# A convolution's bias in its band matrices, LayerNorm's affine part on VectorE, and fewer early query loads

## The chip, the cores and the metric

One core of a Trainium2 chip. The metric is the device time of one execution in microseconds (us), the median over several runs. Engines: TensorE (PE; its weight loads PEld), VectorE (DVE), ScalarE (ACT), GpSimd (POOL) and SyncE (SP), which here issues nearly all transfers; a few are issued by ACT and POOL.

## The reference, cut to what matters

The program is one step of a two-layer hybrid network on 256 prompt tokens and 1024 sample tokens of width 1024. Layer 0 projects the normed input to a convolution branch (A) and a differential attention (B). The change is in branch A:

```python
a = a_u * jax.nn.sigmoid(a_g)                      # 512 channels
a = lax.conv_general_dilated(a, conv_w, ..., feature_group_count=A_W) + conv_b   # 31 taps, one filter per channel
a = jax.nn.silu(layer_norm(a, ln_g, ln_b)) * jax.nn.silu(a_z)
# layer_norm: (x - mean) * rsqrt(var + 1e-6) * g + b over the 512 channels
...
return jnp.concatenate([a, o], axis=-1) @ w_out    # o: the attention's output
```

All tensors are float32; products are made of two parts, a rounded value (`hi`) and what is left of it (`lo`).

## The kernel before, in words

`l0_in` is the input projection of layer 0. Seven groups of 512 weight columns pass over ten tiles of 128 tokens; after each unit, `filler` calls the steps of two generators, so that their work stands between the projection's matmuls: `branch` (the convolution `conv`, then `ln_steps`) and `mod` (the modulation of later stages, on DVE).

The first group writes `a` times 2, as `hi` and `lo`, to the DRAM buffers `AW` (L410 to L420), with zero rows between and around the two sequences (L404 to L408). `conv` takes 64 channels at a time, `q` = 0 to 7. `windows(q)` (L432) makes a tile `X` of 128 partitions: partitions 0 to 63 hold 64 consecutive time steps of `hi`, 64 to 127 those of `lo`, for 42 overlapping windows that start every 32 steps. Four transfers fill it (even and odd windows, `hi` and `lo`), each of 64 rows x 21 windows x 64 channels, on SP's queue. Two `X` tiles take turns (`bufs=2`): the load of window `q+1` is called at `c0 == 8` of window `q` (L463) and has to wait until the matmuls of window `q-1` are through. Each channel's matmul (L471) multiplies its column of `X` with a band matrix of 64 rows x 32 outputs that is built on the host in `_layout` from the 31 taps (L1522 to L1526); an output of the 32 needs 31 steps, so rows 0 to 61 are used and rows 62 and 63 of each half are zero. The band matrices (`rawb`, `band`) of 16 channels are loaded two ahead (`load_taps`, `cut_taps`), on the same queue. The result goes to PSUM, is summed by ACT and DVE (L476, L477) into `cy`, and is stored by ACT's queue to `CV` (L480).

`ln_steps` takes ten tiles of `CV`: `stats` halves the value and adds the bias (L575), takes mean and variance (L577, L579), adds the epsilon (L580), raises to the power -1/2 on POOL (L95) and makes the factor and the offset (L582); `norm` applies them on ACT (L587) and multiplies and adds the affine part on POOL (L588, L589); then come Tanh on ACT (L610) and two products on DVE (L593, L594), and the store to `CAT`. Its tiles take over the memory of the `X` tiles and of `cy`.

`freed0` (L1418) is called in the last weight group: it opens the pool `pre0` on the memory of the first sample tokens' input and loads the keys of head 0 (`l0_keys`) and the queries of groups 1, 2 and 0 of head 0 (`l0_query`, four transfers each), all on SP's queue. `l0_attn` takes those queries at L782 and loads all others when it comes to them, from a pool with three buffers.

The order of the instructions on each engine and queue is made by a planner at build time, from the program's order as priority and estimated durations; each engine and each queue then runs its list in order.

Of the kernel before, what the change touches and what calls it, by code (L numbers as in the profile page):

```python
# [10 lines left out]
F32 = mybir.dt.float32  # L11
F32R = mybir.dt.float32r
BF16 = mybir.dt.bfloat16
AF = mybir.ActivationFunctionType
ALU = mybir.AluOpType
# [8 lines left out]
EPS = 1e-6  # L24
CW0 = 288
CWIN = 42
CROWS = 32 * CWIN + 32
CCH = 64
# [4 lines left out]
def f32(ap):  # L33
    return ap.bitcast(F32)
# [42 lines left out]
class K:  # L77
# [323 lines left out]
    def l0_in(self, ws, raw, wp, cxp, p1, small, acc, pst, mod, freed):  # L401
        nc, a = self.nc, self.a
# [7 lines left out]
        def ug_units(gi):  # L410
# [10 lines left out]

            return [(f"ug{gi}_{t}", self.mm_tok(t), lambda ps, t=t: done(t, ps)) for t in TORD]

        def conv():

# [2 lines left out]
            raws, bands = [], []  # L430

            def windows(q):  # L432
                x = cxp.tile([128, CWIN, CCH], F32R, tag="X", bufs=2, name=f"X{q}")
                cs = slice(q % 4 * CCH, q % 4 * CCH + CCH)
                for o in range(2):
                    for hl in range(2):
                        src = self.AW[q // 4][hl, 32 * o : 32 * o + 32 * CWIN, cs].rearrange("(j r) c -> r j c", r=64)
                        dst = x[hl * 64 : hl * 64 + 64].rearrange("p (j o) c -> p o j c", o=2)[:, o]
                        nc.sync.dma_start(f32(dst), f32(src))
                return x  # L440

# [17 lines left out]
            for q in range(8):  # L459
                y = cxp.tile([CWIN, 32, CCH], F32, tag="cy", bufs=1, name=f"cy{q}")  # L460
                x = xs.pop(0)
                for c0 in range(0, CCH, 8):
# [3 lines left out]
                    for i in range(8):  # L466
                        c = c0 + i
                        if c % 16 == 0:
                            cut_taps()
                        w = bands[4 * q + c // 16]  # L470
# [7 lines left out]
                    if c0 + 8 == CCH:  # L478
                        dst = self.CV[:, q * CCH : q * CCH + CCH].rearrange("(w m) c -> w m c", m=32)
# [3 lines left out]
        def head_units(h):  # L483
# [21 lines left out]
                            nc.sync.dma_start(f32(dst).rearrange("i c t -> (i c) t"), f32(x[qk * 64 : qk * 64 + 64, hl, 0:n]))  # L505

            def vz_done(t, ps):
                v = small.tile([128, 128], F32, tag="vz", name=f"vz{h}_{t}")
                nc.scalar.copy(v, ps[:, 256:384])
                nc.sync.dma_start(self.V0[h, t], v)  # L510
                gz = small.tile([128, 128], F32, tag="gz", name=f"gz{h}_{t}")
                self.silu2(gz, ps[:, 384:512], small, f"z{h}_{t}")
                nc.vector.tensor_tensor(gz, gz, self.subg, ALU.mult)
                nc.sync.dma_start(self.GZ0[h, t], gz)
                return v
# [30 lines left out]
            vz = [(f"v{h}_{t}", self.mm_tok(t, 256), lambda ps, t=t: vz_done(t, ps)) for t in range(NT)]  # L546
# [10 lines left out]
        def ln_steps():  # L557

            con = cxp.tile([128, 3, 512], F32, tag="cy", bufs=1, name="lncon")
            for i, nm in enumerate(("lng", "lnb", "convb")):
                nc.sync.dma_start(con[:, i], a[nm].broadcast_to([128, 512]))
            ws = [cxp.tile([128, CWIN * CCH], F32, tag="X", bufs=2, name=f"lnw{i}") for i in range(2)]
            slots = [w[:, i * 512 : i * 512 + 512] for w in ws for i in range(5)]
# [6 lines left out]

            def stats(t):
                u = us[t % 6]
                nc.vector.scalar_tensor_tensor(u, u, 0.5, con[:, 2], ALU.mult, ALU.add)  # L575
                st = small.tile([128, 6], F32, tag="bn", name=f"bn{t}")
                nc.vector.bn_stats(st, u)  # L577
                mvs[t] = mv = small.tile([128, 4], F32, tag="mv", bufs=3, name=f"mv{t}")
                nc.vector.bn_aggr(mv[:, 0:2], st)  # L579
                nc.vector.tensor_scalar(mv[:, 1:2], mv[:, 1:2], EPS, None, ALU.add)  # L580
                self.rsq(mv[:, 2:3], mv[:, 1:2])
                nc.vector.tensor_scalar(mv[:, 3:4], mv[:, 0:1], mv[:, 2:3], -1.0, ALU.mult, ALU.mult)  # L582

            def norm(t):
                u, mv = us[t % 6], mvs[t]
                nc.sync.dma_start(azs[t % 2], self.AZ[t])
                nc.scalar.activation(u, u, AF.Identity, bias=mv[:, 3:4], scale=mv[:, 2:3])  # L587
                nc.gpsimd.tensor_tensor(u, u, con[:, 0], ALU.mult)  # L588
                nc.gpsimd.tensor_tensor(u, u, con[:, 1], ALU.add)  # L589

            def gate(t):
                u = us[t % 6]
# [661 lines left out]
def build(tc, a):  # L1254
    nc = tc.nc
    k = K(tc, a)
    with ExitStack() as ctx:
# [35 lines left out]
        def right(name):  # L1293
            return tc.alloc_tile_pool(name=name, bufs=1, side="right", **T)
# [36 lines left out]
        with ExitStack() as c1:  # L1331
            hp = pool(c1, "hp0")
            hpr = right("hp0r")
            small = pool(c1, "sm0", 2)
# [77 lines left out]
            cxp = pool(c1, "cx0")  # L1412
# [3 lines left out]
            pre = []  # L1416

            def freed0():  # L1418
                hpr.release()
                p = right("pre0")  # L1420
                pre.extend([[p], k.l0_keys(0, p, 1), {g: k.l0_query(0, g, p, 3) for g in (1, 2, 0)}])

            k.hlb = 1
            k.l0_in(ws, raw, wp, cxp, p1, small, acc, pst, mod, freed0)
# [1 line left out]
        with ExitStack() as c1:  # L1426
# [30 lines left out]
            small = pool(c1, "sm1", 2)  # L1457
            p1 = pool(c1, "p1_1")
            ws = kvw[1] + [k.wsplit(a["wod"][0, j], raw, wp, f"w1_0_{j}") for j in range(k.nkv, KC)]
            pre = []  # L1460
# [22 lines left out]
def _layout(i):  # L1483
    c = np.ascontiguousarray
    p64 = _perm64()
    halves = p64.reshape(2, 32)
    z = {}
# [34 lines left out]
    band = np.zeros((512, 64, 32), np.float32)  # L1522
    for m in range(32):
        band[:, m : m + 31, m] = i["a_conv_w"][0].T
    band = band.reshape(32, 16, 64, 32).transpose(0, 2, 1, 3).reshape(32, 64, 512)
    z["toep"] = c(np.concatenate([band, band], 1))  # L1526
    z["convb"] = c(i["a_conv_b"])
    z["lng"], z["lnb"] = c(i["a_ln_g"]), c(i["a_ln_b"])
    z["lamv"] = c(i["b_lambda"][0])
    z["subg"] = c(i["b_subln_g"])  # L1530
# [10 lines left out]
    for nm, fn in (("ropec", np.cos), ("ropes", np.sin)):  # L1541
        t = fn(ang).astype(np.float32)
        t = np.concatenate([t * np.float32(0.125), t], 1)
        z[nm] = c(t.reshape(8, 128, 64).transpose(1, 0, 2))
    q, kk = np.arange(128)[:, None], np.arange(128)[None]
    t = [fn(ang).astype(np.float32).T for fn in (np.cos, np.sin)]
# [36 lines left out]
```

## Time and profile before

| | |
|---|---|
| median of 3 runs | 1825.25 us (1824.95 to 1827.32) |
| the profiled execution | 1827.64 us, span 1825.9 us |
| mean granted TensorE clock | 0.985 of full speed |
| busy share of the span | PE 95%, PEld 78%, DVE 68%, ACT 53%, POOL 44% |
| convolution's first and last matmul | 139.2 and 405.0 us |
| layer 0's attention, first matmul of its scores | 525.8 us |

The span is what the profile covers, from the first to the last instruction; some 1.7 us of the execution's time lie outside. Busy times of an engine are sums of its instructions. "L471" is line 471 of the kernel before.

### The profile page before, as it was taken

Reading aid. Unit: us, or ns where it says so; the run is one execution under the profiler, and the core shown is the slowest. Engines: PE = TensorE matmul, PEld = TensorE weight load, DVE = VectorE, ACT = ScalarE, POOL = GpSimd, SP = SyncE. Lnnn points to the kernel's source line nnn. Section 1 sums busy time; section 2 is a strip of 40 time slices with the busy share of each in tenths; the row PEclk is TensorE's granted clock in tenths of the full one; section 3 lists DMA queues with packets and bytes.
Section 4 is the critical chain, followed back from the end, with each engine's and each line's share of the span. In section 5 each row is a group of like instructions: output and inputs, shape, how many; then the busy total and the mean of one; then the engine's idle time right before and its main releaser. Section 6 shows DMA issues by size and latency. Waiting matters only on the chain. (4 is left out here: it accounts for less than half of the span.)

```text
span 1825.9 us, 28267 instructions
## 1 busy us (share of the span) xinstructions
PE 1727.1 (95%) x9434; PEld 1421.5 (78%) x9434; DVE 1242.8 (68%) x2935; ACT 974.1 (53%) x2060; POOL 797.3 (44%) x716
## 2 busy tenths in 40 slices
PE   6998999998979899999999999998999999999998
PEld 2787788887767677778887778877888888878886
DVE  7656665675859889935576672118999899999322
ACT  6432334443347678743344533227778788898311
POOL 2321032236637777863237873202343334455332
PEclk9999999999989999999999999999999999999999
DMA  8468878865693332144246345254122114141441
GB/s 299 160 157 196 214 208 185 205 178 167 182 254 93 101 100 88 45 138 162 76 158 194 140 132 156 81 141 103 36 57 58 30 41 107 59 137 61 154 172 58
DMA packets 220278, 241.24 MB, mean 132 GB/s; under 512 B 72128, under 2 KB 154848, under 8 KB 219876
## 3 DMA queue, kind: packets, MB, share of 16 engines
q1 hardware_dynamic: 207476, 233.53, 44.2%
q0 software_dynamic: 1792, 3.15, 0.9%
q10 hardware_dynamic: 10864, 2.75, 0.8%
q8 instruction: 75, 1.23, 0.3%
q14 instruction: 71, 0.58, 0.1%
HBM read 169.08 MB, written 70.28 MB: 131 GB/s over the span
## 5 line engine op out<-in xcount | busy, mean ns | idle before, releaser
L397 ACT ACTIVATE E<-E,mm 128x1536 f32<-128x1536 f32 (+3 forms) x240 | 293.1, 1224 | 71.1 <-DVE E L394 61.4
L270 POOL TENSOR_TENSOR w_w<-raw_w,w_w 128x512 fp32r<-128x512 f32 x88 | 122.9, 1406 | 246.3 <-ACT w_w L269 232.8
L1239 PE MATMUL S<-k1d,q1s 128*128 128x512 f32 (+1 forms) x704 | 206.0, 390 | 4.8 <-DVE E L394 2.1
L372 POOL TENSOR_TENSOR el<-ef,eh 128x512 fp32r<-128x512 f32 x96 | 124.1, 1293 | 188.2 <-DVE eh L371 183.3
L394 DVE TENSOR_SCALAR_CACHE_REDUCE E<-S,mm 128x512 f32<-128x512 f32 x256 | 190.0, 744 | 14.8 <-PE S L799 5.2
L1169 PE MATMUL wt_et<-ident,E 128*128 128x128 f32 x1264 | 187.4, 273 | 3.7 <-DVE om L1192 2.3
L1169 PEld LDWEIGHTS wt_et<-ident,E 128*128 128x128 f32 x1264 | 154.8, 141 | 39.2 <-DVE om L1192 2.7
L368 DVE TENSOR_TENSOR el<-wt_et,eh 128x512 fp32r<-128x512 f32 x220 | 147.0, 682 | 8.3 <-ACT eh L367 7.9
L1239 PEld LDWEIGHTS S<-k1d,q1s 128*128 128x128 f32 x704 | 120.3, 190 | 27.2 <-DVE E L394 7.9
L1164 PE MATMUL pv_pv<-el,v 128*128 128x512 f32 x316 | 139.1, 440 | 0.4 <-POOL el L372 0.2
L367 ACT CAST eh<-wt_et 128x512 fp32r<-128x512 f32 x220 | 123.6, 592 | 26.8 <-PE wt_et L1169 26.2
L799 PE MATMUL S<-kd,qs 128*128 128x512 f32 (+1 forms) x416 | 130.0, 426 | 7.6 <-DVE E L394 6.3
L319 PE MATMUL acc_g<-w_w,hi 128*128 128x512 f32 x336 | 132.3, 394 | 0.0
L318 PE MATMUL acc_g<-w_w,hi 128*128 128x512 f32 x336 | 131.5, 393 | 0.8 <-DVE v L1022 0.7
L320 PE MATMUL acc_g<-w_w,lo 128*128 128x512 f32 x336 | 131.7, 392 | 0.0
L1163 PE MATMUL pv_pv<-eh,v 128*128 128x512 f32 x316 | 128.2, 406 | 0.6 <-DVE eh L371 0.3
L874 PE MATMUL acc_po<-wo,oh 128*128 128x512 f32 x320 | 126.2, 396 | 0.3 <-DVE oy L746 0.3
L875 PE MATMUL acc_po<-wo,oh 128*128 128x512 f32 x320 | 125.2, 392 | 0.0
L394 DVE TENSOR_SCALAR_CACHE_REDUCE E<-S 128x512 f32<-128x512 f32 (+1 forms) x160 | 100.1, 630 | 17.3 <-PE S L1239 9.2
L269 ACT CAST w_w<-raw_w 128x512 fp32r<-128x512 f32 x96 | 58.9, 619 | 94.4 <-DMA raw_w<-in_we 29.5
L878 PE MATMUL acc_po<-wo,ol 128*128 128x512 f32 x320 | 103.2, 394 | 0.0
L799 PEld LDWEIGHTS S<-kd,qs 128*128 128x128 f32 x416 | 70.3, 196 | 28.6 <-DVE E L394 20.4
(295 smaller groups left out, 4570.7 us busy)
## 6 DMA issues: line engine op xcount, KB each, us to landing
rawm_v<-in_wmodt SPq DMA_DIRECT2D x64, 256.0 KB, 3.1
raw_w<-in_we SPq DMA_DIRECT2D x56, 256.0 KB, 3.1
X<-AW SPq DMA_DIRECT2D x32, 336.0 KB, 7.1
qs<-QK SPq DMA_DIRECT2D x80, 128.0 KB, 2.8
ac<-CAT SPq DMA_DIRECT2D x20, 512.0 KB, 4.1
raw_w<-in_wod SPq DMA_DIRECT2D x40, 256.0 KB, 2.6
q1s<-qT SPq DMA_DIRECT2D x40, 256.0 KB, 2.6
xraw_m<-in_wmod SPq DMA_DIRECT2D x32, 256.0 KB, 4.4
```

The lines of the kernel that those rows point to most:

```text
L318: nc.tensor.matmul(ps[:, o:], a, w[:, 0, o:], start=(k == 0), stop=False)
L319: nc.tensor.matmul(ps[:, o:], a, w[:, 1, o:], start=False, stop=False)
L320: nc.tensor.matmul(ps[:, o:], b, w[:, 0, o:], start=False, stop=(k == KC - 1))
L368: nc.vector.tensor_tensor(lo, ps, f32(hi), ALU.subtract)
L394: nc.vector.tensor_scalar(e[:, o : o + w], S, -1.0, init, ALU.mult, ALU.min, accum_out=m[:, i : i + 1])
L397: nc.scalar.activation(e[:, :n], e[:, :n], AF.Exp, bias=init, scale=-1.0, accum_out=s)
L799: nc.tensor.matmul(S, q[:, hl], kd[:, c, kofs + o : kofs + o + n], start=(hl == 0), stop=(hl == 1))
L874: nc.tensor.matmul(po[hn], oh[:, k, :], wo[k][:, 0, s], start=(k == 0), stop=False)
L1163: nc.tensor.matmul(pv, vs, wh, start=(i == 0), stop=False)
L1164: nc.tensor.matmul(pv, vs, wl, start=False, stop=(i == nk - 1))
L1169: nc.tensor.transpose(ps[:, g * 128 : g * 128 + 128], E[g][:, ec : ec + 128], self.ident)
L1239: nc.tensor.matmul(S, qs[:, g, :], kd[hl][:, kc : kc + n], start=(hl == 0), stop=(hl == 1))
```

## The change

The two `X` tiles are made once, before `conv`, and POOL fills partitions 32 to 63 with 2.0 and 96 to 127 with 0.0. A window's transfers now write 62 of the 64 rows of each half, so rows 62 and 63 keep their constants. Row 62 of every band matrix holds the channel's bias, so that the product adds 2 times the bias. `stats` takes mean and variance of the doubled value as it is, with four times the epsilon. The affine part is two operations of DVE on the value, without ACT and POOL: (x - mean) * g, then * factor + b. `vz` and `gz` get a third buffer. `freed0` loads the queries of group 1 alone.

```diff
+        win = [cxp.tile([128, CWIN, CCH], F32R, tag="X", bufs=2, name=f"win{i}") for i in range(2)]
+        for w in win:
+            nc.gpsimd.memset(f32(w[32:64]), 2.0)
+            nc.gpsimd.memset(f32(w[96:128]), 0.0)
+
         def conv():
             raws, bands = [], []
 
             def windows(q):
-                x = cxp.tile([128, CWIN, CCH], F32R, tag="X", bufs=2, name=f"X{q}")
+                x = win[q % 2]
                 cs = slice(q % 4 * CCH, q % 4 * CCH + CCH)
                 for o in range(2):
                     for hl in range(2):
-                        src = self.AW[q // 4][hl, 32 * o : 32 * o + 32 * CWIN, cs].rearrange("(j r) c -> r j c", r=64)
-                        dst = x[hl * 64 : hl * 64 + 64].rearrange("p (j o) c -> p o j c", o=2)[:, o]
+                        src = self.AW[q // 4][hl, 32 * o : 32 * o + 32 * CWIN, cs].rearrange("(j r) c -> r j c", r=64)[0:62]
+                        dst = x[hl * 64 : hl * 64 + 62].rearrange("p (j o) c -> p o j c", o=2)[:, o]
                         nc.sync.dma_start(f32(dst), f32(src))
                 return x
...
-                v = small.tile([128, 128], F32, tag="vz", name=f"vz{h}_{t}")
+                v = small.tile([128, 128], F32, tag="vz", bufs=3, name=f"vz{h}_{t}")
...
-                gz = small.tile([128, 128], F32, tag="gz", name=f"gz{h}_{t}")
+                gz = small.tile([128, 128], F32, tag="gz", bufs=3, name=f"gz{h}_{t}")
...
-            con = cxp.tile([128, 3, 512], F32, tag="cy", bufs=1, name="lncon")
-            for i, nm in enumerate(("lng", "lnb", "convb")):
+            con = cxp.tile([128, 2, 512], F32, tag="cy", bufs=1, name="lncon")
+            for i, nm in enumerate(("lng", "lnb")):
...
             def stats(t):
                 u = us[t % 6]
-                nc.vector.scalar_tensor_tensor(u, u, 0.5, con[:, 2], ALU.mult, ALU.add)
...
-                nc.vector.tensor_scalar(mv[:, 1:2], mv[:, 1:2], EPS, None, ALU.add)
+                nc.vector.tensor_scalar(mv[:, 1:2], mv[:, 1:2], 4 * EPS, None, ALU.add)
                 self.rsq(mv[:, 2:3], mv[:, 1:2])
-                nc.vector.tensor_scalar(mv[:, 3:4], mv[:, 0:1], mv[:, 2:3], -1.0, ALU.mult, ALU.mult)
 
             def norm(t):
                 u, mv = us[t % 6], mvs[t]
                 nc.sync.dma_start(azs[t % 2], self.AZ[t])
-                nc.scalar.activation(u, u, AF.Identity, bias=mv[:, 3:4], scale=mv[:, 2:3])
-                nc.gpsimd.tensor_tensor(u, u, con[:, 0], ALU.mult)
-                nc.gpsimd.tensor_tensor(u, u, con[:, 1], ALU.add)
+                nc.vector.scalar_tensor_tensor(u, u, mv[:, 0:1], con[:, 0], ALU.subtract, ALU.mult)
+                nc.vector.scalar_tensor_tensor(u, u, mv[:, 2:3], con[:, 1], ALU.mult, ALU.add)
...
-                pre.extend([[p], k.l0_keys(0, p, 1), {g: k.l0_query(0, g, p, 3) for g in (1, 2, 0)}])
+                pre.extend([[p], k.l0_keys(0, p, 1), {1: k.l0_query(0, 1, p, 1)}])
...
     for m in range(32):
         band[:, m : m + 31, m] = i["a_conv_w"][0].T
+    band[:, 62] = i["a_conv_b"][0][:, None]
...
-    z["convb"] = c(i["a_conv_b"])
```

## Rows read from the trace of the kernel before

**Rows 1.** The page: busy time of TensorE; GB/s in 40 equal slices of the span.

```profile
PE 1727.1 (95%) x9434; PEld 1421.5 (78%) x9434; DVE 1242.8 (68%) x2935; ACT 974.1 (53%) x2060; POOL 797.3 (44%) x716
...
GB/s 299 160 157 196 214 208 185 205 178 167 182 254 93 101 100 88 45 138 162 76 158 194 140 132 156 81 141 103 36 57 58 30 41 107 59 137 61 154 172 58
```

**Rows 2.** Busy time by stretch: from:to, length, engines, clock, DMA share, GB/s.

```profile
128.00:405.00 277.00, 268.61 (x1698) 231.35 (x1697) 181.19 (x378) 104.72 (x246) 62.74 (x41) 0.99 0.83 198
405.00:500.00 95.00, 84.44 (x483) 73.44 (x483) 68.63 (x120) 33.24 (x84) 60.23 (x45) 0.93 0.60 169
500.00:528.00 28.00, 22.21 (x138) 20.18 (x138) 8.05 (x21) 7.38 (x30) 6.24 (x6) 0.88 0.83 228
528.00:800.00 272.00, 244.20 (x1361) 196.71 (x1360) 239.46 (x607) 197.55 (x407) 197.71 (x170) 0.97 0.36 98
```

**Rows 3.** The window tile X: matmuls, who waited, landing (ns min/median/max, first and last start).

```profile
L471 PE MATMUL tr_cv<-band_band,X x512: 191/239/285, 139.2 to 405.0; 128*42 128x64 f32 x171
...
  PE tr_cv L471: 1.9, 1
...
DMA to landing us min/median/max: 5.7/7.1/8.9
```

**Rows 4.** SP's queue in order of time: start, length, operation (windows 0, 2 and 7).

```profile
127.93 9.45 SPq L439 DMA_DIRECT2D X<-AW  x6
...
172.22 5.68 SPq L439 DMA_DIRECT2D X<-AW  x3
...
350.54 1.48 SPq L439 DMA_DIRECT2D X<-AW  x2
```

**Rows 5.** DMA issues by line: count, KB each, median us to landing.

```profile
X<-AW SPq DMA_DIRECT2D x32, 336.0 KB, 7.1
...
CV<-cy ACTq DMA_DIRECT2D x8, 336.0 KB
...
AW<-z SPq DMA_DIRECT2D x2, 98.0 KB
```

**Rows 6.** Busy time by stretch of 2 us, first and last of four.

```profile
132.00:134.00 2.00, 2.00 (x10) 1.64 (x9) 1.02 (x4) 0.22 (x1) 0.00 (x0) 1.00 1.39 168
...
138.00:140.00 2.00, 0.84 (x12) 0.87 (x12) 0.00 (x0) 0.00 (x0) 0.00 (x0) 1.00 1.38 174
```

**Rows 7.** POOL: the one memset of line 405; the weight cut at 102 us.

```profile
L405 POOL MEMSET z<- x1: 515/515/515, 0.9 to 0.9; 64x512 f32 x1
...
102.13 3.80 POOL L270 TENSOR_TENSOR w_w<-raw_w,w_w 128x512 fp32r<-128x512 f32 x3 [29.21 <-ACT w_w L269]
```

**Rows 8.** LayerNorm's lines: ns min/median/max, first and last start.

```profile
L575 DVE SCALAR_TENSOR_TENSOR lnw<-lnw,lncon x10: 673/682/1747, 423.7 to 474.3; 128x512 f32<-128x512 f32 x10
...
L582 DVE TENSOR_SCALAR mv<-mv x10: 184/202/208, 429.7 to 481.6; 128x1 f32<-128x1 f32 x10
...
L587 ACT ACTIVATE lnw<-lnw,mv x10: 804/816/827, 429.9 to 481.9; 128x512 f32<-128x512 f32 x10
...
L588 POOL TENSOR_TENSOR lnw<-lnw,lncon x10: 1262/1736/1747, 431.2 to 483.6; 128x512 f32<-128x512 f32 x10
...
L589 POOL TENSOR_TENSOR lnw<-lnw,lncon x10: 1275/1544/1744, 433.0 to 487.0; 128x512 f32<-128x512 f32 x10
```

**Rows 9.** TensorE's waits from 400 to 500 us: total, times, longest.

```profile
PE acc_v L318 <- DVE gz L340: 5.5, 1, 5.5
PE acc_c L330 <- ACT nat L527: 4.4, 1, 4.4
```

**Rows 10.** The stage's end in order of time on SP, ACT and TensorE, idle time in brackets.

```profile
499.85 6.93 SPq L683 DMA_DIRECT2D qs<-QK  x9
...
508.07 0.62 ACT L500 CAST ch<-ch 128x512 fp32r<-128x512 f32 x1 [9.59 <-DMA qs<-QK]
...
510.58 4.97 SPq L505 DMA_DIRECT2D QK<-ch  x8
...
512.88 1.11 PE L360 MATMUL tr_st<-ident,hl 128*128 128x128 f32 x4 [5.34 <-DVE hl L357]
```

## The prediction, made before the changed kernel was run

> **What bounds the kernel now.** I read the page's busy line first: TensorE is busy for 95% of the span [rows 1], so time is gained or lost only where it stands idle, and I went on to the stretches that the change touches [rows 2]. From 128 to 405 us runs the convolution, interleaved with the input projection: TensorE is busy for 268.6 of 277 us, at a granted clock of 0.99. From 405 to 500 us LayerNorm runs beside the rest of the projection (84.4 of 95 us busy), from 500 to 528 us the stage ends (22.2 of 28, clock 0.88), and from 528 to 800 us comes the attention of layer 0. So the convolution's stretch is TensorE's own; whatever else it needs is hidden in it, and the question is how far that cover reaches.
>
> What the cover holds is read from the rows of the window tile `X`: its first matmul starts at 139.2 us, its last at 405.0, and a window load takes 5.7 to 8.9 us to land [rows 3]. SP's queue starts the loads of windows 0 and 1 at 127.93 us, of window 2 at 172.22 and of window 7 at 350.54 [rows 4]: (350.54 - 172.22) / 5 = 35.7 us for each window of 64 channels. With two buffers, a window's loads have some 35.7 us before TensorE misses them.
>
> **The window loads, 64 rows cut to 62.** Each of the 32 loads moves 336 KB in runs of 64 channels, 256 bytes: 64 rows x 21 = 1344 packets [rows 5]. Between 132 and 140 us these loads have the DMA engines nearly to themselves: the rate stands at 168 to 174 GB/s (mean of the four slices 172), and the share is 1.38 to 1.39 throughout [rows 6]. That is 10.8 GB/s for each of 16 engines, or 23.8 ns for a packet. The same engines reach 299 GB/s in the first slice of the page, 18.7 GB/s each [rows 1], so in these slices it is the number of packets per engine that counts, not the memory. The level rate without a tail also says that 64 rows are dealt out in equal shares, four rows to an engine.
>
> 62 rows have no such share: 62 = 2 x 31, so whole, equal shares exist for 1, 2, 31 or 62 engines. No row shows how such a load is dealt. The bounds are 16 engines (nothing changes) and 2. The trace's large transfers have 128, 64 or 32 rows; the convolution's stores have 42 and the zero pads of `AW` 15, 32 and 49 [rows 5], for which equal shares use 14, 15, 16 and 7 engines, so no slow one among them would give the dealing away. Since the one dealing that shows is equal [rows 6], I take 2. The Trainium skill, DMA: Bandwidth & Descriptors, section on why a DMA increments its semaphore by 16, states that a transfer runs on the largest number of engines up to 16 that divides the slowest dimension of both sides. By that rule 62 rows give 2 engines and the sum below; by the nearest row, the 64-row load, it would be the 7 us gain of the first rival. No row here shows the rule at work on such a count.
>
> With 2 engines: 62 x 21 / 2 = 651 packets each, x 23.8 ns = 15.5 us a load, 62.0 us for a window's four, where there are 35.7 us. The cover is gone. The other transfers of the stretch use the same two engines: 198 GB/s x 277 us = 54.8 MB, less 32 x 344 kB = 11.0 MB of windows, leaves 5.65 MB in 35.7 us, 0.353 MB per engine, 18.9 us at 18.7 GB/s. At a share of 1.38 an engine has more than one packet in hand, so I count 18.9 / 1.38 = 13.7 us. One window then takes 62.0 + 13.7 = 75.7 us, with TensorE's 35.7 us beside it. The sum: 127.9 + 2 x 62.0 (windows 0 and 1 are loaded back to back) + 6 x 75.7 + 35.7 (the last window's matmuls) = 741.8 us for the end of the convolution, where it is 405.0: **+337 us**. LayerNorm, the output projection and all that follows stand behind it.
>
> The bounds for 2 engines. Below: the packets go at the best rate per engine that the page shows, 256 / 18.7 = 13.7 ns, so 35.7 us a window and 49.4 a cycle: 127.9 + 71.4 + 296.4 + 35.7 = 531, +126 us. Above: SP issues in order, and the six loads from 127.93 us held it for 9.45 us, 1.6 us apiece [rows 4], so a slow load holds back what is queued behind it: the taps of a window's last 16 channels, weights, and the stores that free `vz`, `gz` and `ch`. If none of the projection goes on beside the loads, a cycle is 62.0 + 35.7 = 97.7 us: 127.9 + 124 + 586 + 35.7 = 874, +469 us. What is late next in this case is TensorE itself, waiting in `cv` for `X`, and everything queued on it.
>
> **The constant rows.** Four memsets of 32 partitions x 2688 elements on POOL: the one memset of the trace took 515 ns for 512 elements [rows 7], so some 2.7 us each, 10.8 in all. They stand ahead of the first window load and may delay POOL's weight cuts; POOL is idle for 29.2 us before 102.13 [rows 7], but the tiles' memory may come free later. Between 0 and 10.8 us; I take 0, since POOL is busy for 62.7 of 277 us after that too [rows 2].
>
> **LayerNorm.** DVE loses the bias (L575, 0.68 us median, 1.75 at most) and the small L582 (0.20) and gains two operations of L575's kind, per tile: +0.48 us, +4.8 us over ten. ACT loses L587 (0.82 each, 8.2 us), POOL L588 and L589 (1.74 and 1.54, 33 us) [rows 8]. The chain of a tile, from the power on POOL to the Tanh, loses 0.20 + 0.82 + 1.74 + 1.54 = 4.3 us and gains 1.4. TensorE's idle time in this stretch is one wait of 5.5 us for DVE's `gz` and one of 4.4 us for ACT's `nat` [rows 9], both behind DVE, which gets more work from this and not less. The bounds are a loss of 4.8 (all of DVE's addition lands on the path) and a gain of 9.9; I take a gain of 2. The third buffer of `vz` and `gz` and the dropped load of `convb` lie in the same stretch and are in that number.
>
> **The queries.** SP issues nine query loads from 499.85 us, 6.93 us long; ACT's cast of `ch` waits 9.59 us until 508.07 for them, SP comes to the stores of `ch` at 510.58 only, and TensorE idles 5.34 us ahead of 512.88 [rows 10]. Eight of twelve loads leave this place, 8 x 0.77 = 6.2 us of SP. They come back in the attention's first 20 us, behind its own loads on SP; if one is late there, the price is an issue queue of 6.2 us. So between a gain of 5.3 and a loss of 6.2; I take a gain of 5, since groups 2 and 0 are wanted only after group 1.
>
> **Sum.** +337 - 2 - 5 = +330 us on the profiled execution's 1827.64: 2157.6. That execution lies 2.4 us above the median of the runs (1825.25), so **2155 us**.
>
> **Rivals.** (1) *The rows are spread all the same, and the kernel gets faster.* Place: the window loads. With k engines a window takes 4 x 1302 x 23.8 ns / k = 124 us / k; it hides while that is below 35.7 - 13.7 = 22 us, so from 6 engines on. Then only the 7 us remain: 1818 us, 1812 to 1829 by the bounds of the small parts. For it: today's even spread [rows 6]. Against it: an uneven count would have to be dealt with a remainder, of which the trace has no case. 9%. (2) *The loads are slow, but work that does not need the convolution is moved ahead.* Attention of layer 0 (528 to 800 us) needs no LayerNorm. Engines 0 and 1 would have 496 us of windows and the other transfers of 128 to 800 us: (54.8 - 11.0 + 169 x 0.095 + 228 x 0.028 + 98 x 0.272 = 93 MB) / 16 / 18.7 GB/s = 311 us, / 1.38 = 225 us; 721 us in a stretch of 672, so +49, and LayerNorm's first tiles behind it, some 30: about 1900 us. Against it: TensorE, ACT and SP run their queues in order, and the attention's tiles take over memory of this stage. 8%. (3) *Each window load also waits for the constant rows*: excluded, they are written once, ahead of the loop.
>
> **Chances.** The forecast's case has 83%. The range takes in its lower bound, rival (2) and its upper bound: 1895 to 2290 us; some 1 in 7 is left out, rival (1) and the rest of the tails. A measurement of this kernel tells 0.2%, 3.7 us, from no change. Rival (1) gives faster 6% and the same 3%; all else is slower, 91%.
>
> **What would show it.** Right: the landing of `X` rises from 7 to over 15 us a load; the starts of the window loads lie some 76 us apart, not 35.7; TensorE's waits in `cv` for `X` grow from 1.9 us [rows 3] to some 300; the DMA share in the stretch falls, since 14 engines stand idle; LayerNorm shows no line on ACT ahead of its Tanh; the idle time ahead of 512.88 us shrinks. Wrong: if the loads still land in 7 us, or the spacing stays at 36 us, the loads were spread over more engines and rival (1) holds; if the spacing is some 50 us, the packets were faster than in rows 6; if it nears 98, nothing ran beside the loads.

## The result, and the profile after

The changed kernel takes **2041.09 us** (median of 4 runs, 2039.83 to 2046.93) beside 1825.78 us (median of 4) for the kernel before: ratio 1.1174, 95% interval 1.1157 to 1.1192. The profiled execution took 2040.00 us with a span of 2037.8, which is 211.9 us more than before. The forecast was 2155 us in a range of 1895 to 2290: the sign and the place were right, the size was 114 us too high.

| us | before | after | |
|---|---|---|---|
| TensorE busy in the span | 1727.1 | 1749.0 | +22 |
| TensorE idle in the span | 98.8 | 288.8 | +190 |
| last matmul of the convolution | 405.0 | 632.5 | +227.5 |
| from there to the first scores of layer 0 | 120.8 | 113.9 | -6.9 |
| from there to the first matmul of the output projection | 274.6 | 267.4 | -7.2 |
| all the rest of the span | 1025.5 | 1024.0 | -1.5 |

So all of the loss lies ahead of the convolution's last matmul, and what lies behind it is 15.6 us shorter. The page of the kernel after, busy times and the slices of 2.5%:

```profile
PE 1749.0 (86%) x9434; PEld 1438.5 (71%) x9434; DVE 1221.2 (60%) x2935; ACT 964.6 (47%) x2050; POOL 777.3 (38%) x700
...
PE   6963665683849889999899999999899999999998
...
PEclk9986877886869999999999999999999999999999
DMA  8332453333545675242162464535401211333351
GB/s 298 129 96 51 139 164 102 92 91 99 143 126 168 199 205 132 84 126 77 42 219 76 145 191 144 135 111 141 123 27 34 78 36 44 98 94 114 111 186 52
```

From the third slice to the twelfth TensorE's digits fall to 3 to 8, its granted clock to 6 to 8, and the transfers move 51 to 164 GB/s; before, the same slices moved 157 to 254 GB/s [rows 1]. One stretch deeper: busy time by stretch of the kernel after (from:to, length, PE, PEld, DVE, ACT, POOL, clock, DMA share, GB/s). The first three lines span the convolution and answer to the first of [rows 2].

```profile
128.00:300.00 172.00, 84.33 (x413) 67.80 (x413) 56.03 (x125) 25.91 (x56) 13.04 (x8) 0.72 0.36 108
300.00:460.00 160.00, 105.96 (x632) 91.73 (x630) 48.96 (x97) 32.66 (x68) 21.18 (x14) 0.82 0.34 93
460.00:633.00 173.00, 105.05 (x654) 91.92 (x655) 69.19 (x154) 46.18 (x125) 31.20 (x19) 0.76 0.46 127
633.00:747.00 114.00, 102.65 (x609) 89.53 (x608) 69.32 (x134) 33.09 (x103) 36.45 (x31) 0.97 0.64 188
747.00:1014.00 267.00, 242.97 (x1368) 195.93 (x1367) 234.25 (x612) 197.78 (x409) 193.27 (x170) 0.98 0.37 103
```

TensorE is busy for 295.3 of the 505 us of the convolution, at clocks of 0.72 to 0.82. The tile of the windows, now named `win` (shortest, median and longest of one in ns, first and last start), answers to [rows 3] and [rows 7]:

```profile
L477 PE MATMUL tr_cv<-band_band,win x512: 191/240/310, 164.2 to 632.5; 128*42 128x64 f32 x171
L445 SPq DMA_DIRECT2D win<-AW x32: 258/9098/13480, 124.1 to 567.0; - x32
L426 POOL MEMSET win<- x2: 2334/2337/2340, 108.2 to 113.0; 32x2688 f32 x2
```

SP now stands at half of the window loads for 9.1 us or more; before, six of them took it 9.45 us together [rows 4]. The tile has no landing time in this profile, so the rate takes its place. In short stretches with only window loads under way, the kernel after shows (same columns):

```profile
132.00:134.00 2.00, 2.00 (x9) 1.32 (x7) 0.35 (x1) 0.00 (x0) 0.00 (x0) 1.00 0.16 36
134.00:136.00 2.00, 0.04 (x1) 0.00 (x0) 0.00 (x0) 0.00 (x0) 0.00 (x0) 1.00 0.16 32
136.00:138.00 2.00, 0.00 (x0) 0.00 (x0) 0.00 (x0) 0.00 (x0) 0.00 (x0) 0.69 0.16 36
138.00:140.00 2.00, 0.00 (x0) 0.00 (x0) 0.00 (x0) 0.00 (x0) 0.00 (x0) 0.50 0.16 36
140.00:150.00 10.00, 0.00 (x0) 0.00 (x0) 0.00 (x0) 0.00 (x0) 0.00 (x0) 0.50 0.16 36
...
200.00:210.00 10.00, 4.25 (x17) 3.47 (x18) 6.02 (x15) 1.09 (x3) 0.00 (x0) 0.50 0.86 293
```

36 GB/s at a share of 0.16 stand where [rows 6] have 168 to 174 at 1.38. From 136 to 150 us every engine is idle and only the transfers go on; from 200 to 210 us, when the loads are through, 293 GB/s flow. After TensorE's last matmul at 134 us its granted clock reads 1.00, 0.69 and then 0.50, the lower of its two levels (1.2 GHz).

SP's queue in order of time in the kernel after (start, length, operation), which answers to [rows 4]:

```profile
124.06 66.42 SPq L445 DMA_DIRECT2D win<-AW  x8
...
228.68 30.80 SPq L445 DMA_DIRECT2D win<-AW  x4
259.58 9.03 SPq L263 DMA_DIRECT2D raw_w<-in_we  x1
...
296.47 13.79 SPq L445 DMA_DIRECT2D win<-AW  x2
310.31 9.13 SPq L560 DMA_DIRECT2D AZ<-az  x1
319.49 0.28 SPq L445 DMA_DIRECT2D win<-AW  x1
319.87 10.93 SPq L263 DMA_DIRECT2D rawb_band<-in_toep  x1
...
546.12 30.12 SPq L445 DMA_DIRECT2D win<-AW  x4
```

Window 2's loads start at 228.68 and window 7's at 546.12: (546.12 - 228.68) / 5 = 63.5 us a window, where it was 35.7. The transfer behind the window loads, whatever it is (a weight at 259.58, a store at 310.31, the taps at 319.87), holds SP for another 9 to 11 us. That is why the waits carry other names than the window's. What the engines waited for from 128 to 640 us (total, times, longest):

```profile
...
PE tr_cv L477 <- DVE cy L483: 126.4, 14, 30.4
...
ACT band_band L269 <- DMA rawb_band<-in_toep: 93.0, 7, 29.5
DVE cy L483 <- ACT cy L482: 92.6, 17, 33.4
ACT w_w L269 <- DMA raw_w<-in_we: 91.4, 10, 29.4
```

Read from the last line up: ACT waits for weights and taps that SP has not issued yet, so its share of `cy` is late, DVE's too, and TensorE waits 126.4 us for a place in PSUM. One such case in order of time, on SP, ACT and TensorE (idle time in brackets):

```profile
390.74 9.13 SPq L263 DMA_DIRECT2D rawb_band<-in_toep  x1
...
402.43 0.62 ACT L269 CAST band_band<-rawb_band 128x512 fp32r<-128x512 f32 x1 [18.74 <-DMA rawb_band<-in_toep]
...
404.61 0.58 PE L477 MATMUL tr_cv<-band_band,win 128*42 128x64 f32 x5 [16.05 <-DVE cy L483]
```

SP comes to these taps behind three window loads that it began at 367.66 us; ACT stands 18.74 us for them, and TensorE 16.05 us for `cy`. TensorE's own waits from 100 to 640 us show the window by name just once:

```profile
PE tr_cv L477 <- DMA win<-AW: 30.2, 1, 30.2
PE acc_az L318 <- ACT w_w L269: 29.5, 1, 29.5
PE acc_c L330 <- ACT w_w L269: 22.9, 2, 19.5
```

### The profile page after: what moved, and what is told of

Read it like the earlier page. It is cut to its first block, busy times and chain, and to the rows that moved or that the text cites. A ratio compares the mean times of both kernels' runs of the same rounds, so it can differ in the third digit from the quotient of the medians.

```text
span 2037.8 us, 28251 instructions
## 1 busy us (share of the span) xinstructions
PE 1749.0 (86%) x9434; PEld 1438.5 (71%) x9434; DVE 1221.2 (60%) x2935; ACT 964.6 (47%) x2050; POOL 777.3 (38%) x700
## 5 line engine op out<-in xcount | busy, mean ns | idle before, releaser
L270 POOL TENSOR_TENSOR w_w<-raw_w,w_w 128x512 fp32r<-128x512 f32 x88 | 124.0, 1422 | 432.6 <-ACT w_w L269 386.1
L477 PE MATMUL tr_cv<-band_band,win 128*42 128x64 f32 x512 | 47.3, 241 | 156.6 <-DVE cy L483 126.4
L477 PEld LDWEIGHTS tr_cv<-band_band,win 128*42 128x42 f32 x512 | 46.1, 166 | 164.0 <-DVE cy L483 121.0
L269 ACT CAST w_w<-raw_w 128x512 fp32r<-128x512 f32 x96 | 58.8, 620 | 161.0 <-DMA raw_w<-in_we 101.7
```

## The experiments

The theory: a load of 62 rows is dealt to 2 DMA engines, which are slow by their number alone, and everything else of the change is a small gain. Its rivals: another part of the change makes the loss; the rows matter by something else than their divisors; or the loss is only a queue that the loads hold, and goes away where they are issued elsewhere. "Before" beside each run is the kernel before on the same chip, 1826.66 to 1828.30 us in the median.

| kernel | us | ratio, 95% interval | convolution ends at |
|---|---|---|---|
| 62-row loads alone | 2060.07 | 1.1265 [1.1238, 1.1292] | 633.6 |
| 63 rows | 1829.53 | 1.0010 [0.9992, 1.0029] | 424.0 |
| 63 rows, two buffers | 1817.62 | 0.9955 [0.9938, 0.9971] | 406.1 |
| 31 + 31 rows | 2327.43 | one execution | 918.2 |
| 48 + 14 rows | 1826.49 | 0.9989 [0.9974, 1.0005] | 415.7 |
| 32 + 30 rows, two buffers | 1813.45 | 0.9937 [0.9914, 0.9960] | 402.6 |
| 62 rows, spread on SP's queue | 2055.95 | 1.1238 [1.1206, 1.1270] | 647.0 |
| 62 rows, issued by POOL | 2210.15 | 1.2085 [1.2059, 1.2112] | 796.5 |
| LayerNorm on VectorE alone | 1819.25 | 0.9948 [0.9926, 0.9970] | 404.8 |
| queries alone | 1820.57 | 0.9957 [0.9943, 0.9971] | 404.8 |
| both, and third buffers | 1819.14 | 0.9945 [0.9924, 0.9966] | 413.4 |
| both, two buffers | 1814.15 | 0.9937 [0.9921, 0.9953] | 405.8 |

**The loads alone.** The kernel before, with the two tiles that last through the convolution, their rows 32 to 63 and 96 to 127 cleared to zero ahead of it, and 62-row loads; bias, LayerNorm and queries as before. Of the edit, the loads:

```diff
-                        src = self.AW[q // 4][hl, 32 * o : 32 * o + 32 * CWIN, cs].rearrange("(j r) c -> r j c", r=64)
-                        dst = x[hl * 64 : hl * 64 + 64].rearrange("p (j o) c -> p o j c", o=2)[:, o]
+                        src = self.AW[q // 4][hl, 32 * o : 32 * o + 32 * CWIN, cs].rearrange("(j r) c -> r j c", r=64)[0:62]
+                        dst = x[hl * 64 : hl * 64 + 62].rearrange("p (j o) c -> p o j c", o=2)[:, o]
```

> The kernel before with one part of the change alone: the two window tiles are made once, POOL clears their rows 32 to 63 and 96 to 127 to zero, and a window's four loads write 62 rows instead of 64 (rows 62 and 63 stay zero, as the bands are there). Theory A, two engines: 62 rows go to 2 of 16 DMA engines, and this alone makes the loss. In the trace of after the four loads of a window take 37 us on two engines (36 GB/s), and the last convolution matmul starts 227 us later than before; here the same, and the gains that after shows behind the convolution (some 15 us) are missing: 1825.8 + 227 = 2053 us, 2035 to 2070. Rival B, another part: if the constant rows that the tiles carry, the bias in the bands or the shifted order make the loss, this kernel stays within 20 us of 1826.

2060.07 us. The loads and the lasting tiles make the whole loss; the other parts of the change give 2060 - 2041 = 19 us of it back (by the ratios, 0.9% or 17 us).

**One row more.** The change with 63 rows in a load, and the bias in row 63 of the bands. 63 = 9 x 7, so that nine engines get equal shares.

```diff
-                        src = self.AW[q // 4][hl, 32 * o : 32 * o + 32 * CWIN, cs].rearrange("(j r) c -> r j c", r=64)[0:62]
+                        src = self.AW[q // 4][hl, 32 * o : 32 * o + 32 * CWIN, cs].rearrange("(j r) c -> r j c", r=64)[0:63]
-                        dst = x[hl * 64 : hl * 64 + 62].rearrange("p (j o) c -> p o j c", o=2)[:, o]
+                        dst = x[hl * 64 : hl * 64 + 63].rearrange("p (j o) c -> p o j c", o=2)[:, o]
...
-    band[:, 62] = i["a_conv_b"][0][:, None]
+    band[:, 63] = i["a_conv_b"][0][:, None]
```

> The changed kernel with one size changed: loads of 63 rows, and the bias in row 63 of the bands instead of row 62. Theory A, whole equal shares on at most 16 engines: 63 = 9 x 7, so 9 engines, 7 x 21 = 147 packets each; four loads are 588 packets per engine, 8.4 us at the 14.2 ns that two engines show, 14.0 us at the 23.8 ns that sixteen show, both hidden behind 35.7 us of TensorE. The convolution ends near 405 us again, and what after gains behind it is left: 6.9 us up to the attention, 7.2 in it, 1.5 later, so 1826 - 15 = 1811 us, 1803 to 1822. Rival B, any count that 16 does not divide is slow (or the constant rows are): 2000 us or more. Rival C, the remaining parts give nothing without the slow loads: 1822 to 1830.

1829.53 us: one row more is worth some 212 us, with the memsets, the lasting tiles, LayerNorm and the queue as in the change, so none of these makes the loss by itself. The size was off: a gain of 0.9% was expected, and there is none. Where it went shows in the run with two buffers, below.

**Two engines or one.** The same 62 rows as two loads of 31 each. 31 is prime.

```diff
-                        src = self.AW[q // 4][hl, 32 * o : 32 * o + 32 * CWIN, cs].rearrange("(j r) c -> r j c", r=64)[0:62]
-                        dst = x[hl * 64 : hl * 64 + 62].rearrange("p (j o) c -> p o j c", o=2)[:, o]
-                        nc.sync.dma_start(f32(dst), f32(src))
+                        for r0, r1 in ((0, 31), (31, 62)):
+                            src = self.AW[q // 4][hl, 32 * o : 32 * o + 32 * CWIN, cs].rearrange("(j r) c -> r j c", r=64)[r0:r1]
+                            dst = x[hl * 64 + r0 : hl * 64 + r1].rearrange("p (j o) c -> p o j c", o=2)[:, o]
+                            nc.sync.dma_start(f32(dst), f32(src))
```

> The whole change with each window load cut into two of 31 rows. A prime count has only 1 or 31 equal shares, so each of the 64 loads goes to one engine: 31 x 21 = 651 packets of 14.2 ns, 9.25 us. If all go to the same engine and one after the other: the 62-row loads' 296 us become 592 us, a stretch with window loads alone moves 18 GB/s at a share of 0.08, and the time is about 2041 + 296 = 2340 us. If the two halves go to two engines side by side: as with 62 rows, 2041 us and 36 GB/s. If a load is dealt out unevenly over many engines: 1820 to 1830 us and over 120 GB/s.

2327.43 us where 2340 were expected. Its stretches with window loads alone:

```profile
150.00:160.00 10.00, 0.00 (x0) 0.00 (x0) 0.00 (x0) 0.00 (x0) 0.00 (x0) 0.50 0.08 18
200.00:210.00 10.00, 8.33 (x44) 6.84 (x45) 2.28 (x4) 1.95 (x4) 0.00 (x0) 0.70 0.08 19
```

18 GB/s at a share of 0.08 is half of 36 at 0.16, as one engine in place of two would give. No row names the engines; their number is read from the shares, 0.08, 0.16 and, with 63 rows, 0.71 (below), which stand as 1 to 2 to 9. The Trainium skill, DMA: Bandwidth & Descriptors, section "Why a DMA increments its semaphore by 16 and not by 1", gives the engine count as the largest number up to 16 that divides the slowest dimension of both sides, and says that a transfer of SP's takes the lowest-numbered engines. This case agrees with both: 64, 63, 62 and 31 rows moved 172, 160, 36 and 18 GB/s, and two loads of 31 rows did not run side by side.

**Many engines, two buffers.** First the 63-row kernel with `vz` and `gz` back at two buffers.

```diff
-                v = small.tile([128, 128], F32, tag="vz", bufs=3, name=f"vz{h}_{t}")
+                v = small.tile([128, 128], F32, tag="vz", bufs=2, name=f"vz{h}_{t}")
...
-                gz = small.tile([128, 128], F32, tag="gz", bufs=3, name=f"gz{h}_{t}")
+                gz = small.tile([128, 128], F32, tag="gz", bufs=2, name=f"gz{h}_{t}")
```

> The whole change with 63 rows in each window load (9 engines by equal whole shares) and vz and gz at two buffers as before. If the third buffers cost time: ratio about 0.996, 1821 us. If they do not, and the nine engines' slower loads ahead of the convolution give back what the other parts gain: about 1.001, 1830 us.

1817.62 us, ratio 0.9955, against 1.0010 with three buffers; the intervals don't meet. TensorE's waits from 128 to 426 us, with three buffers:

```profile
PE tr_cv L477 <- DVE cy L483: 13.9, 8, 5.6
PE tr_st L360 <- DVE hl L357: 3.1, 1, 3.1
PE tr_cv L477 <- DMA win<-AW: 2.8, 1, 2.8
```

and with two:

```profile
PE tr_cv L477 <- DVE cy L483: 6.4, 6, 1.5
PE acc_az L318 <- ACT w_w L269: 1.7, 1, 1.7
PE tr_cv L477 <- DMA win<-AW: 1.2, 1, 1.2
```

With the third buffers TensorE waits longer in the convolution, which ends at 424.0 us and not at 406.1. That the third buffers cost the time here is shown; by which instruction of the new order is not. (The first of these executions lies 9 us above its kernel's median, the second 3 us below, so part of the difference is theirs.)

Then the 62 rows in two loads that both use many engines: 48 + 14 rows, with three buffers, and 32 + 30, with two (both edits against the kernel with 31 + 31).

```diff
-                        for r0, r1 in ((0, 31), (31, 62)):
+                        for r0, r1 in ((0, 48), (48, 62)):
```

```diff
-                        for r0, r1 in ((0, 31), (31, 62)):
+                        for r0, r1 in ((0, 32), (32, 62)):
...
-                v = small.tile([128, 128], F32, tag="vz", bufs=3, name=f"vz{h}_{t}")
+                v = small.tile([128, 128], F32, tag="vz", bufs=2, name=f"vz{h}_{t}")
...
-                gz = small.tile([128, 128], F32, tag="gz", bufs=3, name=f"gz{h}_{t}")
+                gz = small.tile([128, 128], F32, tag="gz", bufs=2, name=f"gz{h}_{t}")
```

> The changed kernel with each load of 62 rows cut in two, of 48 and of 14 rows: 64 loads where there were 32. Theory A: 48 rows go to 16 engines and 14 to 14, at most 63 + 21 = 84 packets per engine and pair, as the 64 rows before; the loads are hidden and the time is that of the 63-row loads, 1811 us, plus up to 2 us for SP, which issues 32 more loads at 0.6 us (19 us in all, in a stretch where SP waits most of the time): 1803 to 1824. Rival B, a number of rows below 64 is what is slow: 2000 us or more.

1826.49 us with 48 + 14 rows: the loss is mended and nothing gained, with three buffers.

> The whole change with each window load cut into two, of 32 and 30 rows, and vz and gz at two buffers as before. Theory (the loss is only the dealing of 62 rows, and the rest of the change is worth some 9 us): the halves go to 16 and 15 engines, window loads alone move over 120 GB/s, the convolution ends near 415 us, and the ratio is 0.992 to 0.996, 1812 to 1819 us. Rival (64 loads instead of 32, with smaller shares each, give back what the rest gains): ratio 0.998 to 1.001, as with 48 and 14 rows. A third (30 rows are not dealt to 15 engines): under 60 GB/s in every second load and over 1900 us.

1813.45 us with 32 + 30 rows, ratio 0.9937: the first expectation. The convolution ends at 402.6 us, before the old 405.0. Two microseconds with window loads alone, in 63 rows with two buffers, then 32 + 30 rows, then 48 + 14 (one kernel a fence):

```profile
132.00:134.00 2.00, 2.00 (x10) 1.37 (x8) 0.21 (x1) 0.00 (x0) 0.00 (x0) 1.00 0.71 162
```

```profile
132.00:134.00 2.00, 1.67 (x13) 1.22 (x12) 0.00 (x0) 0.00 (x0) 0.00 (x0) 1.00 1.32 169
```

```profile
132.00:134.00 2.00, 1.06 (x5) 0.53 (x3) 0.00 (x0) 0.00 (x0) 0.00 (x0) 1.00 1.36 134
```

Nine engines move nearly what sixteen do. Why 48 + 14 rows move less than 32 + 30 at nearly the same share was not tried.

**Where the loads are issued.** First: the four loads of a window apart, each behind a load of taps.

```diff
-                        nc.sync.dma_start(f32(dst), f32(src))
+                        if hl + o == 0 or len(part) > 1:
+                            nc.sync.dma_start(f32(dst), f32(src))
+                        else:
+                            with self.tc.issue_after(self.tap):
+                                nc.sync.dma_start(f32(dst), f32(src))
...
-                    if c0 == 8 and q < 7:
-                        xs.append(windows(q + 1))
+                    if c0 % 16 == 8 and q < 7:
+                        x1 = windows(q + 1, (c0 // 16,))
...
```

> The changed kernel, 62-row loads on SP as in the change, but a window's four loads no longer stand together on SP's queue: the first is called at the window's second step, the others at its fourth, sixth and eighth, each queued behind the taps called just before. In after the four together hold SP for 30 us, and taps, weights and stores come after them. Theory A1, the pace of two engines: they need 37 us for a window and 14 to 19 us for their part of all other transfers, 51 to 56 us where TensorE needs 35.7; spreading changes little more than the order: last convolution matmul at 124 + 37 + 7 x 53 + 36 = 568 us against 632 in after, 1950 to 2000 us. Theory A2, the order: two engines nearly keep up and only the bunching hurts; a window takes 40 us, the last matmul comes at 477 us, below 1900 us.

2055.95 us, slower than 2041 and outside both expectations. Its SP queue shows why:

```profile
305.43 0.26 SPq L446 DMA_DIRECT2D win<-AW  x1
305.78 10.59 SPq L567 DMA_DIRECT2D AZ<-az  x1
...
328.96 0.29 SPq L449 DMA_DIRECT2D win<-AW  x1
330.63 9.31 SPq L261 DMA_DIRECT2D rawm_v<-in_wmodt  x1
```

A single window load is issued in 0.3 us, and the transfer behind it stands for 9 to 11 us, as long as the load takes on its two engines (9.25 us, below). So the queue, as these rows show it, has room for little more than one such load, and spreading them only spreads the standstill. TensorE's waits from 100 to 640 us change their names and hardly their sum (209.8 and 215.1 us): for `win` they grow from 30.2 to 98.1 us, for `cy` they fall from 126.4 to 58.8.

Second: the window loads on POOL's queue.

```diff
-                        nc.sync.dma_start(f32(dst), f32(src))
+                        nc.gpsimd.dma_start(f32(dst), f32(src))
```

> The changed kernel with the window loads issued by POOL instead of SP, 62 rows as in the change. It tells whether the loss comes from the loads' own rate or from what waits behind them on SP. Theory A1, the rate: POOL's loads run on two engines too, 37 us a window against 35.7 us of TensorE, the loads set the pace and the time stays above 1900 us. Theory A2, the held queue: two engines are just fast enough, and with SP free (8 to 9 us for each load in after) taps, weights and stores come in time; the loss falls below 40 us, to 1815 to 1865. If POOL's way of issuing deals 62 rows to more engines, the landing of a load falls from 37 us for four to below 15, and the time is about 1811 to 1835, with POOL's weight cuts delayed by the issuing.

2210.15 us. POOL in order of time:

```profile
388.05 4.01 POOL L445 DMA_DIRECT2D win<-AW  x1 [17.62 <-issue]
408.56 4.01 POOL L445 DMA_DIRECT2D win<-AW  x1 [16.51 <-issue]
```

Each load costs POOL 4.0 us, 16.5 to 17.6 us pass before it, and the weight cuts wait behind. A load lands 15.2 to 21.3 us after its issue, more than the 9.25 us that it takes by SP's rate. This run says that POOL is no way out; it doesn't say what the engines' rate alone would cost, since POOL too stands between the loads. How much of the change's loss is the rate of two engines and how much the standing queue, no run here tells apart.

**The small parts.** The kernel before with LayerNorm's affine part on VectorE alone, then with one pair of queries alone, then with both edits, with and without the third buffers. In all of them the loads have 64 rows and the bias is added in LayerNorm.

```diff
-                nc.vector.tensor_scalar(mv[:, 3:4], mv[:, 0:1], mv[:, 2:3], -1.0, ALU.mult, ALU.mult)
...
-                nc.scalar.activation(u, u, AF.Identity, bias=mv[:, 3:4], scale=mv[:, 2:3])
-                nc.gpsimd.tensor_tensor(u, u, con[:, 0], ALU.mult)
-                nc.gpsimd.tensor_tensor(u, u, con[:, 1], ALU.add)
+                nc.vector.scalar_tensor_tensor(u, u, mv[:, 0:1], con[:, 0], ALU.subtract, ALU.mult)
+                nc.vector.scalar_tensor_tensor(u, u, mv[:, 2:3], con[:, 1], ALU.mult, ALU.add)
```

> The kernel before with LayerNorm's affine part on VectorE alone (bias still added there). The prediction's term: a gain of 2 us, bounds a loss of 4.8 and a gain of 9.9; here VectorE carries 0.7 us a tile more. Ratio 0.996 to 1.002; if POOL and ACT were what held the stretch behind the convolution, a gain of 6 to 10 us, ratio 0.995.

1819.25 us, -9.5 us by the ratio. The middle of LayerNorm in this kernel, and then in the kernel before (busy time by stretch: PE, PEld, DVE, ACT, POOL):

```profile
445.00:465.00 20.00, 18.44 (x93) 14.75 (x92) 20.00 (x31) 7.75 (x27) 14.08 (x10) 1.00 0.81 258
```

```profile
445.00:465.00 20.00, 15.64 (x76) 12.95 (x75) 14.94 (x20) 6.92 (x21) 20.00 (x15) 0.86 0.69 217
```

POOL was busy without a gap and DVE had 5 us to spare; now it is the other way about, and TensorE gets 2.8 us more work into the same 20 us. Its wait for ACT's `nat` falls from 4.4 us [rows 9] to 0.8. The first scores come at 517.7 us, 8.1 earlier. The edit takes work from POOL and from ACT at once; which of the two gave the gain was not isolated.

```diff
-                pre.extend([[p], k.l0_keys(0, p, 1), {g: k.l0_query(0, g, p, 3) for g in (1, 2, 0)}])
+                pre.extend([[p], k.l0_keys(0, p, 1), {1: k.l0_query(0, 1, p, 1)}])
```

> The kernel before with the queries alone: freed0 loads those of group 1 only. The prediction's term: a gain of 5 us (5.3 us of TensorE's idle time ahead of 512.88 us), bounds a gain of 5.3 and a loss of 6.2. From after's trace, where the attention itself takes 7.2 us less: the freed memory may also let the attention's tiles start earlier, then 7 to 10 us. Ratio 0.994 to 0.998; rival, the loads are only moved: 1.000.

1820.57 us, -7.9 us, but in another place than forecast. The scores start at 526.3 us (525.8 before), and TensorE's waits from 400 to 560 us still have the old one:

```profile
PE tr_st L360 <- DVE hl L357: 5.5, 1, 5.5
...
PE S L799 <- DMA qs<-QK: 3.2, 1, 3.2
```

The attention itself is shorter, 265.3 us from the first scores to the output projection and not 274.6, although it now waits 3.2 us for a query. What in it the early loads had held up was not isolated.

> The kernel before, its convolution and its 64-row loads untouched (the bias stays in LayerNorm), with the three other parts of the change: affine part on VectorE, third buffers of vz and gz, one pair of queries early. If what after gains behind the convolution (15.6 us, from its trace) comes from these parts: 1828 - 15 = 1813 us on the chip of the last runs, ratio 0.990 to 0.994. VectorE has one operation more per tile than in after, +0.7 us over ten tiles each at worst 7 us. Rival: they give nothing without the constant rows: ratio 0.998 to 1.002.

> The kernel before with two parts of the change alone: the affine part of LayerNorm on VectorE, and one pair of early queries; window loads of 64 rows, bias added in LayerNorm, two buffers for vz and gz. Theory (the two gains of 8.1 and 9.5 us are separate pieces of idle time, and the third buffers spoilt the run that had both): ratio about 0.990, 1811 us. Rival (the two gains are the same idle time, or the planner's order gives one of them back): about 0.9945, 1819 us, as with either part alone.

1819.14 us with third buffers and 1814.15 without: ratios 0.9945 and 0.9937, whose intervals overlap almost wholly. The sum of the two parts would be 0.9905, outside the second's interval (0.9921 to 0.9953) but uncertain itself by some 0.0026, from the intervals of its two parts. That the two gains are partly the same time is likely by this, and not shown. In the profiled execution without third buffers the scores start at 520.0 us and the attention takes 268.8: 5.8 us are gained in each place, where each part alone gained 8.1 and 9.3. At 64 rows the third buffers cost nothing that can be told, although the convolution ends 7.6 us later with them.

## Why the prediction was right in sign and too large

**Where the bound is.** Right: TensorE's stretch with the convolution lost its cover, and the whole of the loss lies there.

**The dealing of 62 rows.** Right, and shown by rate and share: 36 GB/s at 0.16 for two engines, 18 at 0.08 for one with 31 rows, 160 at 0.71 for nine with 63.

**23.8 ns for a packet.** This is the term that failed. It was 172 GB/s [rows 6] divided by 16 engines, and the sentence behind it said that the packets per engine count, "not the memory". One, two and nine engines move 18, 36 and 162 GB/s: 18.0 GB/s an engine each time, or 256 / 18.0 = 14.2 ns a packet. Sixteen would move 288 at that rate and move 168 to 174, so the 10.8 GB/s of [rows 6] were no property of an engine: sixteen together slowed each other on these packets. The share says so too: with sixteen engines a packet is under way for 1.38 x 16 x 256 / 172 = 33 ns, with two for 0.16 x 16 x 256 / 36 = 18 ns. What they shared is not shown. A load takes 651 x 14.2 = 9.25 us, not 15.5, a window 37.0 us, not 62.0.

The forecast's lower bound, 13.7 ns from the 18.7 GB/s of [rows 1], came close to this by luck. That slice is an average over other packets (5612 of its 7503 have 2 KB or more) and over microseconds in which the engines move nearly nothing; inside it the trace before has (busy time by stretch):

```profile
4.00:12.00 8.00, 0.59 (x2) 0.09 (x3) 5.22 (x11) 6.38 (x12) 2.21 (x4) 1.00 1.02 390
```

390 GB/s are 24 GB/s an engine, so 18.7 was not the best rate either.

**13.7 us for the other transfers.** Too small. A cycle of 63.5 us leaves 26.5 us beside the 37.0 of loads. The forecast counted the time that the other transfers take on the engines; in fact SP's queue stands while a load is on its way, and what it holds back, weights and taps above all, is what TensorE then misses. The upper bound had named this, but for the whole of the 35.7 us; TensorE was busy for 58% of the convolution, so part of its work did go on.

**The sum.** Against the forecast's 741.8 us: the start and windows 0 and 1 make 23.2 us less (228.7, not 251.9), five cycles 61.0 less (63.5, not 75.7), and from window 7's loads to the last matmul it takes 86.4 us, not 75.7 + 35.7 = 111.4. Together 109 us less, 632.5. The first of these hides two parts: the first eight loads need 8 x 9.25 = 74 us, not 124, but 30 us then pass until window 2's loads start. The two wrong terms also pull opposite ways. With 14.2 ns alone put right, the sum would be 127.9 + 74.0 + 6 x 50.7 + 35.7 = 541.8 us, 91 us too early; with 26.5 us alone, 127.9 + 124.0 + 6 x 88.5 + 35.7 = 818.6 us, 186 us too late. That the one error made up for part of the other is luck. The loss also holds a term that the forecast lacked: 22 us more of TensorE's busy time, with the granted clock at 0.72 to 0.82 in the three stretches where it was 0.99 [rows 2].

**The constant rows.** Right at nothing: the four memsets take 9.4 us from 108.2 on, and the first window load starts at 124.06, where it was 127.93 [rows 4].

**LayerNorm.** Gain of 2 forecast, some 9 measured in the kernel before with this part alone, near the end of the bounds (9.9). The step that failed is "both behind DVE, which gets more work": DVE was not full there, POOL was, and this stood in a stretch narrower than the 95 us of [rows 2] that I read (60.2 of 95 us on POOL, 68.6 on DVE).

**The queries.** Gain of 5 forecast, 8 measured with this part alone, for another reason: the idle time ahead of 512.88 us [rows 10], which was the argument, stays at 5.5 us in the kernel with this edit alone.

**The rivals.** (1), spread rows, fell for 62 rows, but its number was good for nine engines with two buffers, 1818 us forecast and 1817.6 measured; with the change's third buffers it was 1829.5. Its threshold, hidden from 6 engines on, was worked out with the 23.8 ns and was not tried. (2) fell: no scores start before 746.4 us. (3) stayed excluded.

**What would show it.** The spacing came out at 63.5, between the 50 of faster packets and the 98 of nothing beside the loads: the packets were faster, and less ran beside the loads than forecast. The 300 us of waits for `X` by name came out as 30.2; the waits for `cy` (126.4) and for weights (29.5 and 22.9) are the same delay one or two engines further on.

## What to carry to other kernels

Before the partition count of a transfer is trimmed, look at its divisors: 62 rows put these loads on two engines, and the change lost 215 us by them, while 63 rows, or 32 + 30, cost nothing that could be measured. A rate measured with all engines at work is a total; how fast a few of them are has to be read from a stretch where they are not sharing, with packets of the same size. A slow transfer is charged to whatever is queued behind it, so its price stands in the waits for other names; and gains in neighbouring stages are measured together, since 9.5 and 7.9 us made 11.5 here.

The best versions here are the change with loads of 32 + 30 rows and two buffers (1813.45 us) and the kernel before with LayerNorm on VectorE and one pair of queries (1814.15 us), both at 0.9937 of before. So the bias in the bands, with the loads that it needs, brings nothing that can be measured.

## What the runs showed of the hardware that was not expected

- One DMA engine, by the shares, moved 18 GB/s in packets of 256 bytes, two 36 and nine some 160, while sixteen stopped at 168 to 174 together.
- A transfer behind one slow load on SP's queue stood for 9 to 11 us, about the 9.25 us of that load.
- POOL needed 4.0 us to issue a load of 62 x 21 runs, and 16.5 to 17.6 us passed before each in the rows shown; SP issued one in 0.3 us where none was on its way.
- With TensorE idle from 134 us, its granted clock read 1.00, then 0.69, then 0.50 (the lower level) in three stretches of 2 us, and it was still 0.50 from 200 to 210 us with TensorE busy for 4.25 of 10 us.
